# Reordering the passage into the first seven-product group of a two-layer encoder kernel

## The chip, the cores and the metric

The kernel runs on one core of one Trainium2 chip. The metric is the device time of one execution in microseconds, the median of several; smaller is better.

## The reference

Two layers, 256 tokens, model width 1024, float32 throughout. Each layer is a macaron: half a SwiGLU, a mixer of two attention groups, half a SwiGLU.

```python
for l in range(DEPTH):                      # DEPTH = 2, D_MODEL = 1024, D_FF = 2816
    x = x + 0.5 * swiglu(rms_norm(x, ffn1_norm[l]), w_gate1[l], w_up1[l], w_down1[l])
    h = rms_norm(x, mix_norm[l])
    qa, ka, va, qb, kb, vb = split(h @ w_in[l])
    x = x + concat(windowed_gqa_sink(...), differential_attention(...)) @ w_out[l]
    x = x + 0.5 * swiglu(rms_norm(x, ffn2_norm[l]), w_gate2[l], w_up2[l], w_down2[l])
return rms_norm(x, final_norm)
# swiglu(h) = (silu(h @ w_gate) * (h @ w_up)) @ w_down
```

So there are four SwiGLU blocks, called here F1 and F2 (layer 0) and F3 and F4 (layer 1), with a mixer between F1 and F2 and between F3 and F4. They hold nearly all of the arithmetic.

## The kernel before

**Matmuls in pieces.** Every float32 operand is cut into a high part, rounded to the matmul's format, and a low part, the rest; a product is three matmuls (high·high, low·high, high·low). A weight block of 4x128 rows by 512 columns is one *step*. It is loaded on SyncE's queue into one of six buffers (tag `raw`, `N_RAW = 6`) and then cut in two halves of 128x1024; each half, called a *split*, is one ScalarE cast (the high part) and one VectorE subtraction (the low part). Splits are numbered 2i and 2i+1 for step i. `emit_split` issues them; a raw buffer is given back when its second split has been done.

**Seven products for eight.** The hidden width is taken in groups of 512 columns, n = 0 to 4, and a rest of 256. A plain group multiplies two token halves by gate and up weights, each in two halves of the rows: eight products. For groups in `sevens`, `by_seven` uses a Strassen-like scheme with seven products. With a, d the two row halves of the gate block and b, c those of the up block, it needs the blocks a, d, c, b+c, a+b, a+b+c and a+b+c+d, and four sums of x (`make_sums`: s1, s2, b0_ and v, each with a high and a low part). F1 uses it for groups 2 to 4, the others for groups 1 to 4. Weight sums come about in two ways: `gather(k, to)` is a DMA on GpSimd's queue that reads block k from memory again and adds it into the buffer of block `to`; `plus(x, to)` is two VectorE additions of 128x1024 (tile `raw<-raw,raw`).

**Order.** Outside the attention part everything is kept in program order on each engine. The order is written by hand, by a planner: `weights()` hands out the next step and first calls `ahead(n)`, which issues all splits up to number n, the additions that lie between them, and the loads that now find a free buffer. n is `2 * i + look[0] - less`; `look[0]` is 8 or 7 in group 1. The columns of a step are handed out in two inner halves (`Split.part`); when a product reaches the second, `ahead` is called for one more split, unless the step was asked for with `held=True`. So the order of ScalarE and VectorE work is that of the calls of `weights()` in the source.

**Group 1 in F2, F3 and F4** (steps counted from the start of the SwiGLU block; group 0 uses steps 0 to 3): step 4 is a, 5 is d, 6 is the first half of the down projection of group 0, 7 is c, 8 is b+c, 9 is a+b, 10 is a+b+c, 11 is a+b+c+d, 12 is the other down half. Group 2 follows with step 13 (its a), 14 (its b+c) and so on. `by_seven` on the branch for g = 1 makes p1 (step 4), transposes the first half of the hidden tile `h` into `hT` (`turn`, tile `s`: TensorE transposes, a ScalarE cast, a VectorE subtraction), runs one part of `make_sums`, makes p2 (step 5), transposes the second half of `h`, runs the next part of `make_sums`, forms g0 = p1 + p2 and its silu, and goes on to the down projection (step 6), p3 (step 7), m7 (step 8), p5, p6 and p4 (steps 9 to 11) and step 12. Two VectorE instructions at the end of the group turn its products into the next `h`; the next group transposes it after its own first two products.

**Group 1 in F1** is the plain branch of the loop in `ffn`. There `make_sums` runs in five parts, one at each `next(sums)`: s1 and s2; their high parts; the low parts, b0_ and v; the high parts of b0_ and v; the low parts of these. v (tile `v`) is needed by the second product of group 2.

**Holding additions.** `issue(add)` keeps a gather back in `pending` while `hold[0]` is true, and `flush()` releases all. hold is set near the end of a SwiGLU block (`ffn_end`) and of the mixer, and flush comes after the statistics of the next norm have been issued (`norm.late(2)`, `take_x(2)`), so that GpSimd computes the norm's factor `r` before it takes up additions.

Of the kernel before, what the change touches and what calls it, by code (L numbers as in the profile page):

```python
# [12 lines left out]
ALU = mybir.AluOpType  # L13
# [21 lines left out]
def trunk(ctx: ExitStack, tc: tile.TileContext, x, n1, g1, u1, d1, nm, w_in, sink,  # L35
# [79 lines left out]
    def seven(wg, wu, c0, downs, first):  # L115

        a, b, c, d = [object() for _ in range(4)]  # L120
        w = {a: rows(wg, c0, 512, 0, 4), b: rows(wu, c0, 512, 0, 4), c: rows(wu, c0, 512, 4, 4), d: rows(wg, c0, 512, 4, 4)}

        def load(k):
            return lambda t: [(t, w[k])]

        def gather(k, to):
            def add():
                pool.dma_start(raws[to], w[k], accum_op=ALU.add)
            return add

        def plus(x, to):
            def prep():
                for h in (0, 2):
                    x_, t_ = [raws[i][:, h:h + 2] for i in (x, to)]
                    dve.tensor_tensor(t_, t_, x_, op=ALU.add)
            return prep

        bc = Step(4, 512, load(b), key=b, behind=gather(c, b))
        rest = [Step(4, 512, load(d), key=d, free=[]), Step(4, 512, load(c), key=c, free=[]), downs[0]]
        steps = [rest[0], rest[2], rest[1], bc] if first else [bc] + rest  # L140
        steps[0].prep = lambda: issue(gather(b, a))
        return [Step(4, 512, load(a), key=a, free=[])] + steps + [
                Step(4, 512, None, src=a, free=[]),
                Step(4, 512, None, prep=plus(c, a), src=a, free=[c]),
                Step(4, 512, None, prep=plus(d, a), src=a, free=[a, d]),
                downs[1]]

    def emit_dma(i):
        s = specs[i]
        raws[s.key] = raw = wp.tile([P, s.kn, s.n], F32, tag="raw", bufs=N_RAW, name=nm_("raw"))  # L150
        for dst, src in s.moves(raw):
            if i > 1:
                sp.dma_start(dst, src)  # L153
            else:
                for k in range(s.kn):
                    sp.dma_start(dst[:, k:k + 1], src[:, k:k + 1])
                    yield
        if s.behind is not None:
            issue(s.behind)


    pending, hold = [], [True]

    def issue(add):
        pending.append(add)
        if not hold[0]:
            flush()

    def flush():
        hold[0] = False  # L170
        while pending:
            pending.pop(0)()

# [73 lines left out]
    def weights(less=0, held=False):  # L247

        i = at["use"]
        at["use"] += 1  # L250
        if i > 1:
            ahead(2 * i + look[0] - less)
        w = loaded[i]
        w.held = held
        return w
# [179 lines left out]
    norm = Norm(0)  # L435
# [137 lines left out]
    class Residual:  # L573
# [5 lines left out]
        def add(self, h, t, c=None):  # L579
            a, b = (0, 512) if c is None else (c * 256, c * 256 + 256)  # L580
            xv = xk[:, t, h * 512 + a:h * 512 + b]
            dve.tensor_tensor(xv, xv, self.accs[h][t][:, a:b], op=ALU.add)
# [15 lines left out]
    def ffn(norm, aside=None, before=None, final=False, sevens=SEVEN[1]):  # L598
# [21 lines left out]
        def prod(xo, w):  # L620
            acc = bank()
            for k in range(4):
                hi, lo = w.part(k)
                xh, xl = xo(k)
                pe.matmul(acc, lhsT=xh, rhs=hi, start=k == 0, stop=False)
                pe.matmul(acc, lhsT=xl, rhs=hi, start=False, stop=False)
                pe.matmul(acc, lhsT=xh, rhs=lo, start=False, stop=k == 3)
            return acc

        def by_seven(h, g, sums):  # L630


            flat = lambda: tmp().rearrange("p a n -> p (a n)")

            def put(o, x, y, op):
                dve.tensor_tensor(o, x, y, op=op)
                return o

            m1, m7 = flat(), flat()
            if g > 1:  # L640
                act.copy(m1, prod(norm.quarter(0, 0), weights()))
                act.copy(m7, prod(norm.summed(3), weights(held=True)))
                hT = turn(h, 2)
                p2 = prod(norm.quarter(0, 1), weights())
                g0 = put(flat(), p2, m1, ALU.add)
                p3 = prod(norm.summed(2), weights())
                silu(g0, g0, 0)
                down(hT, g - 1, 0, weights())
            else:
                p1 = prod(norm.quarter(0, 0), weights())  # L650
                hT = turn(h, (0,))
                next(sums, None)
                w = weights()
                act.copy(m1, p1)
                p2 = prod(norm.quarter(0, 1), w)
                hT += turn(h, (1,))
                next(sums, None)
                w = weights()
                g0 = put(flat(), p2, m1, ALU.add)
                silu(g0, g0, 0)  # L660
                down(hT, 0, 0, w)
                p3 = prod(norm.summed(2), weights())
                act.copy(m7, prod(norm.summed(3), weights()))
            h = blk(F32)
            p5 = prod(norm.summed(0), weights())
            late = g == max(sevens)
            p6 = prod(norm.summed(1), weights(look[0] - 5 if late else 0, late))
            u2 = put(flat(), p6, m1, ALU.subtract)
            u3 = put(m7, m7, u2, ALU.add)
            p4 = prod(norm.quarter(1, 1), weights(look[0] - 4 if late else 0, late))  # L670
            g1 = put(m1, p4, u3, ALU.subtract)
            w = weights(look[0] - 3 if late else 0)
            silu(g1, g1, 1)
            put(u3, u3, p5, ALU.subtract)
            put(u2, u2, p5, ALU.subtract)
            put(u2, u2, p3, ALU.add)
            up(h, u2, g0, 0)
            up(h, u3, g1, 1)
            down(hT, g - 1, 1, w)
            return h  # L680

        def turn(hs, n):
            out_ = []
            for i in (range(n) if isinstance(n, int) else n):
                sl = halves(bank())
                for c in range(2):
                    for t in range(2):
                        pe.transpose(sl[:, c, t * P:(t + 1) * P], hs[:, t, (2 * i + c) * P:(2 * i + c + 1) * P], ident)
                hb = blk()
                split(hb, sl)  # L690
                out_.append(hb)
            return out_
# [3 lines left out]
        def down(hT, g, h, w):  # L696
            tokens(accs[h], [None] * (2 * g) + hT, w, 4 * g, last=(FC - 1, G4 - 1) if final and h else FC - 1)
# [14 lines left out]
        w = weights()  # L712
# [16 lines left out]
        for n in range(1, NGRP):  # L729
            if n in sevens:  # L730
                look[0] = IN_FFN + min(sevens) - n if before is not take_x else IN_MIX - (n == NGRP - 1)
                h = by_seven(h, n, sums)
                continue
            sums = norm.make_sums()
            gs = [bank(), bank()]
            tokens(gs, norm.xs, weights(), 0)
            hT = turn(h, 2)
            norm.copies()
            tokens(gs, norm.xs, weights(), 4)
            g = gate(gs)  # L740
            next(sums, None)
            us = [bank(), bank()]
            for k0 in (0, 4):
                tokens(us, norm.xs, weights(), k0)
                next(sums, None)
            h = hidden(g, us)
            for hh in range(2):
                down(hT, n - 1, hh, weights())
                next(sums, None)

        gu = [bank(), bank()]
        tokens(gu, norm.xs, weights(), 0)
# [14 lines left out]
    def ffn_end(parts, last):  # L767

        accs, hT, rest = parts
        hT = [None] * (2 * (NGRP - 1)) + hT  # L770
        hE = []
        look[0] = IN_MIX
        hold[0] = True
        w = {0: weights()}

        def group(h, order, a=None, c=slice(None), first=0):
            tokens(a or accs[h], hT, w[h], G4, first=first, last=last[h], order=order, cols=c)

        def tail(h, order=BY_TOKENS, a=None, c=slice(None)):
            tokens(a or accs[h], [None] * (2 * NGRP) + hE, w["rest"], 4 * NGRP, last=last[h], order=order, cols=c, h=h)  # L780

        group(0, [(k, t) for k in range(3) for t in range(2)])
        hE.extend(rest())
        group(0, [(3, t) for t in range(2)])
        w["rest"] = weights()
        w[1] = weights(2)
        return group, tail
# [20 lines left out]
    def mix(l, norm, nxt_norm):  # L808
# [215 lines left out]
        def out_part(w, k0, h, order=None):  # L1024
            tokens(accs[h], oT, w, k0, range(2), order=order, h=h)

        hold[0] = True
        for k0 in (0, 2, 4):
            w = weights()
            for h in range(2):  # L1030
# [112 lines left out]
```

## Time and profile before

| | |
|---|---|
| time, median of 3 runs | 942.56 us (942.45 to 946.13) |
| the profiled execution's own time | 946.32 us |
| its span, first to last instruction | 944.5 us |
| mean granted TensorE clock | 0.987 |
| TensorE busy | 916.6 us, 4696 matmuls |
| VectorE busy | 807.4 us, 1125 instructions |
| ScalarE busy | 590.6 us, 917 instructions |
| GpSimd busy | 65.3 us, 83 instructions |
| moved by DMA | 200.87 MB, mean 213 GB/s |

The profile is of one execution, in microseconds from its first instruction. Rows of a timeline give start, duration, engine, line, operation, output and input tiles (without buffer numbers), shapes, count and, in brackets, the idle time of the engine before it and what ended it. Nearly all instructions are issued through one helper at line 50, so tiles tell them apart: `w<-raw` is a split's cast (ACT) or subtraction (DVE), `s<-ps,s` the low part of `hT`, `q` and `v` are sums of x, `ps` is a PSUM bank. PE is TensorE, DVE VectorE, ACT ScalarE, POOL GpSimd, SPq SyncE's queue. The table of waits gives the time in total, the count and the longest. The table of stretches gives length, busy time of each engine with its count, granted TensorE clock, DMA share and rate. A row of DMA issues ends with the time from issue to landing. F1 lies at about 6 to 190 us of the span, F2 at 291 to 480, F3 at 481 to 662 and F4 at 763 to the end.

### The profile page before, as it was taken

The page shows a single profiled execution, that of the slowest core. Times are in us where ns is not written, and L with a number is a line of the kernel's source. Part 1 is how long each engine was busy: PE and PEld are TensorE (multiplying, and loading weights), DVE is VectorE, ACT ScalarE, POOL GpSimd, SP SyncE. Part 2 cuts the span into 40 slices and gives each one's busy share as a digit, 9 for nine tenths or more (in the row PEclk, how much of TensorE's full clock was granted, in tenths as well). Part 3 has the DMA queues.
Part 4 walks back from the last instruction along what each step waited for, and adds up shares of the span by engine and source line. Part 5 has one row for each costly group of instructions (what it writes and reads, how often), then busy time and mean ns, then how long its engine had stood idle before and what let it go on. Part 6 is the DMA issues. An engine that isn't in the chain of part 4 may idle for free.

```text
span 944.5 us, 12605 instructions
## 1 busy us (share of the span) xinstructions
PE 916.6 (97%) x4696; PEld 770.1 (82%) x4696; DVE 807.4 (85%) x1125; ACT 590.6 (63%) x917; POOL 65.3 (7%) x83
## 2 busy tenths in 40 slices
PE   8989999999999899999998999999999998999997
PEld 6778887899888688888886888888998886888886
DVE  6757999969885899999878999997788669999995
ACT  7835575647765765675484666665577485666661
POOL 0400010000000100100010010000001010010011
PEclk9998999999999999999998999999999999999999
DMA  9985897927434796897759897978472358898831
GB/s 341 353 209 135 266 279 252 271 90 223 135 110 158 179 283 192 255 294 247 262 145 220 242 275 206 275 256 235 119 237 91 133 137 221 254 262 227 247 146 45
DMA packets 114061, 200.87 MB, mean 213 GB/s; under 512 B 3662, under 2 KB 31376, under 8 KB 114000
## 3 DMA queue, kind: packets, MB, share of 16 engines
q1 hardware_dynamic: 96528, 166.74, 52.4%
q0 software_dynamic: 16096, 31.75, 18.7%
q10 hardware_dynamic: 1376, 1.57, 0.5%
q8 instruction: 37, 0.61, 0.3%
q14 instruction: 24, 0.20, 0.1%
HBM read 199.00 MB, written 1.05 MB: 212 GB/s over the span
## 4 chain that ended last, share of the span: by engine, by line
PE 71%; DMA 12%; DVE 7%; issue 6%; ACT 2%; POOL 0%; SPq 0%; ACTq 0%; POOLq 0%; DVEq 0%
PE ps L50 71%; DMA raw<-in_ffn_w_up_dram 10%; DVE w L50 4%; ACT w L50 1%; DMA raw<-in_ffn_w_gate_dram 1%; DVE raw L50 1%; DVE tmp L50 1%; DVE s L50 1%; DMA xk<-in_x_dram 1%; ACT s L50 0%; ACT junk L50 0%; ACT tmp L50 0%; DVE q L50 0%; POOL rb L50 0%; SPq L153 0%
## 5 line engine op out<-in xcount | busy, mean ns | idle before, releaser
L50 PE MATMUL ps<-w,s 128*128 128x512 f32 (+1 forms) x2574 | 608.0, 393 | 13.9 <-DVE s L50 12.7
L50 PEld LDWEIGHTS ps<-w,s 128*128 128x128 f32 x2574 | 480.8, 190 | 116.2 <-DVE s L50 15.0
L50 DVE TENSOR_TENSOR w<-raw,w 128x1024 fp32r<-128x1024 f32 (+1 forms) x458 | 483.4, 1099 | 48.4 <-ACT w L50 47.4
L50 ACT CAST w<-raw 128x1024 fp32r<-128x1024 f32 (+1 forms) x458 | 409.7, 952 | 124.2 <-DVE raw L50 85.1
L50 PE MATMUL ps<-w,q 128*128 128x512 f32 x540 | 127.6, 390 | 0.0
L50 PEld LDWEIGHTS ps<-w,q 128*128 128x128 f32 x540 | 101.7, 188 | 21.3
L50 PE MATMUL ps<-s,w 128*128 128x256 f32 x672 | 84.0, 285 | 0.0
L50 PEld LDWEIGHTS ps<-s,w 128*128 128x128 f32 x672 | 81.7, 191 | 1.1
L50 DVE TENSOR_TENSOR raw<-raw,raw 128x1024 f32<-128x1024 f32 x60 | 70.5, 1216 | 0.0
L50 POOL DMA_DIRECT2D raw<-in_ffn_w_up_dram x30 | 38.9, 1350 | 368.3 <-DVE w L50 127.5
L50 ACT ACTIVATE s<-ps,gcol 128x256 fp32r<-128x256 f32 (+1 forms) x80 | 31.3, 479 | 46.6 <-PE ps L50 45.0
L50 ACT ACTIVATE tmp<-tmp,r 128x512 f32<-128x512 f32 x30 | 21.7, 722 | 50.1 <-DVE tmp L50 50.1
L50 PE MATMUL ps<-w,v 128*128 128x512 f32 x180 | 45.9, 405 | 3.2 <-DVE v L50 3.2
L50 PEld LDWEIGHTS ps<-w,v 128*128 128x128 f32 x180 | 35.2, 196 | 11.1 <-DVE v L50 3.6
L50 PE MATMUL ps<-ident,s 128*128 128x128 f32 x304 | 41.3, 276 | 0.3 <-DVE s L50 0.3
L50 PEld LDWEIGHTS ps<-ident,s 128*128 128x128 f32 x304 | 35.9, 142 | 6.8 <-issue 1.0
L50 DVE TENSOR_TENSOR s<-ps,s 128x512 fp32r<-128x512 f32 x44 | 28.6, 682 | 10.5 <-ACT s L50 10.5
L50 ACT COPY tmp<-ps 128x512 f32<-128x512 f32 x34 | 19.9, 584 | 27.2 <-PE ps L50 25.6
L50 ACT CAST s<-ps 128x512 fp32r<-128x512 f32 x44 | 24.3, 591 | 20.2 <-PE ps L50 20.2
L50 ACT ACTIVATE s<-s,negm 128x256 f32<-128x256 f32 x64 | 31.9, 500 | 6.6 <-DVE negm L50 6.4
L50 DVE TENSOR_TENSOR tmp<-ps,tmp 128x512 f32<-128x512 f32 x49 | 33.4, 682 | 1.6 <-PE ps L50 1.6
L50 DVE SCALAR_TENSOR_TENSOR s<-ps,gcol,s 128x256 fp32r<-128x256 f32 x48 | 20.3, 478 | 14.8 <-ACT s L50 14.7
(106 smaller groups left out, 405.6 us busy)
## 6 DMA issues: line engine op xcount, KB each, us to landing
raw<-in_ffn_w_down_dram SPq DMA_DIRECT2D x44, 1024.0 KB, 6.5
raw<-in_ffn_w_gate_dram SPq DMA_DIRECT2D x39, 1024.0 KB, 6.5
raw<-in_ffn_w_up_dram SPq DMA_DIRECT2D x39, 1024.0 KB, 5.1
raw<-in_ffn_w_up_dram POOLq DMA_DIRECT2D x30, 1024.0 KB, 11.8
raw<-in_w_in_dram SPq DMA_DIRECT2D x14, 1024.0 KB, 5.4
raw<-in_ffn_w_gate_dram SPq DMA_DIRECT2D x8, 512.0 KB, 6.6
raw<-in_ffn_w_up_dram SPq DMA_DIRECT2D x8, 512.0 KB, 7.6
raw<-in_w_in_dram SPq DMA_DIRECT2D x8, 512.0 KB, 5.6
```

The source lines that it names most:

```text
L50: ins = issue(*a, **k)
```

## The change

Four edits, in four places.

1. In `by_seven` for g = 1, p1 and p2 ask for their steps with `weights(3, True)`: three splits fewer are issued before each product and none in its middle. The call of `weights()` for step 6 moves behind g0 and its silu, and g0 moves ahead of the last part of `make_sums`. Splits 15 to 20 and the additions for step 10 (with the one for split 17, the load of group 2's b) thus stand later in program order: split 15 after the first half of `hT`, the others behind the second half of `hT`, g0 and silu.
2. `hold` gets levels. The gather of c into b ("behind" a load) is kind 2 and is held only at the start of the kernel; the gather of b into a is kind 1 and is held as before.
3. In the plain group (F1, group 1), `next(sums)` is called once more, right after `norm.copies()`, so each part of `make_sums` runs one call earlier.
4. There, the call after the second down half is left out, since nothing remains to be done.

```diff
-        steps[0].prep = lambda: issue(gather(b, a))
+        steps[0].prep = lambda: issue(gather(b, a), 1)
...
         if s.behind is not None:
-            issue(s.behind)
-    pending, hold = [], [True]
-    def issue(add):
-        pending.append(add)
-        if not hold[0]:
-            flush()
+            issue(s.behind, 2)
+    pending, hold = [], [2]
+    def issue(add, kind):
+        if kind <= hold[0]:
+            pending.append(add)
+        else:
+            add()
     def flush():
-        hold[0] = False
+        hold[0] = 0
...
             else:
-                p1 = prod(norm.quarter(0, 0), weights())
+                p1 = prod(norm.quarter(0, 0), weights(3, True))
                 hT = turn(h, (0,))
                 next(sums, None)
-                w = weights()
+                w = weights(3, True)
                 act.copy(m1, p1)
                 p2 = prod(norm.quarter(0, 1), w)
                 hT += turn(h, (1,))
+                g0 = put(flat(), p2, m1, ALU.add)
                 next(sums, None)
-                w = weights()
-                g0 = put(flat(), p2, m1, ALU.add)
                 silu(g0, g0, 0)
-                down(hT, 0, 0, w)
+                down(hT, 0, 0, weights())
...
             norm.copies()
+            next(sums, None)
             tokens(gs, norm.xs, weights(), 4)
...
                 down(hT, n - 1, hh, weights())
-                next(sums, None)
+                if hh == 0:
+                    next(sums, None)
...
         look[0] = IN_MIX
-        hold[0] = True
+        hold[0] = 1
```

More of the change, by code (lines that the diff above doesn't have):

```diff
@@ L1025, in out_part @@
             tokens(accs[h], oT, w, k0, range(2), order=order, h=h)
-        hold[0] = True
+        hold[0] = 1
         for k0 in (0, 2, 4):
```

## The prediction

> **What bounds the kernel now.** I read the page's first part, then what TensorE waited for, then its timeline, and last the timelines of the engine that it waited for. On the page, TensorE is nearly always busy:
>
> ```profile
> PE 916.6 (97%) x4696; PEld 770.1 (82%) x4696; DVE 807.4 (85%) x1125; ACT 590.6 (63%) x917; POOL 65.3 (7%) x83
> ```
>
> The longest entry of its waits is for VectorE, tile `s`, the low parts of hT:
>
> ```profile
> PE ps L50 <- DVE s L50: 13.0, 7, 3.1
> ```
>
> Its timeline shows where. In F1, group 2's second product (right operand `v`) starts and stops:
>
> ```profile
> 67.37 0.39 PE L50 MATMUL ps<-w,v 128*128 128x512 f32 x1
> 70.96 5.06 PE L50 MATMUL ps<-w,v 128*128 128x512 f32 x11 [3.20 <-DVE v L50]
> 77.17 2.99 PE L50 MATMUL ps<-w,s 128*128 128x512 f32 x12
> ```
>
> In F2, group 1's down projection stops twice, and F3 and F4 repeat it. The two last rows are transposes of a hidden tile: group 2's and, two groups on, group 4's.
>
> ```profile
> 322.18 0.48 PE L50 MATMUL ps<-w,s 128*128 128x512 f32 x1
> 324.45 3.06 PE L50 MATMUL ps<-w,s 128*128 128x512 f32 x12 [1.79 <-DVE s L50]
> 330.07 4.13 PE L50 MATMUL ps<-w,s 128*128 128x512 f32 x11 [2.56 <-DVE s L50]
> 334.03 2.88 PE L50 MATMUL ps<-w,q 128*128 128x512 f32 x12
> 358.51 1.03 PE L50 MATMUL ps<-ident,s 128*128 128x128 f32 x8
> 420.17 1.04 PE L50 MATMUL ps<-ident,s 128*128 128x128 f32 x8
> ```
>
> A wait costs more than itself. The stretches show the granted clock (the first figure behind the five engines) at half after each:
>
> ```profile
> 71.00:72.00 1.00, 1.00 (x3) 0.81 (x4) 1.00 (x1) 0.00 (x0) 0.00 (x0) 0.50 0.00 0
> 330.00:332.00 2.00, 1.93 (x5) 1.55 (x6) 2.00 (x4) 0.00 (x0) 0.69 (x1) 0.50 0.74 129
> ```
>
> So F1 lost between 67.37 and 77.17: 9.80 us for twelve matmuls (2.99 by the row at 77.17) and eight transposes (1.03 by the row at 358.51), that is 5.8 too many, of which 3.2 were the wait and 2.6 the slow clock. F2 lost 334.03 - 322.18 = 11.85 us for 24 matmuls, worth 2 x 2.99: 5.9 too many.
>
> Whether that can be had depends on VectorE, which TensorE waits for. Its timeline in F2, from split 15 on:
>
> ```profile
> 320.31 3.49 DVE L50 TENSOR_TENSOR w<-raw,w 128x1024 fp32r<-128x1024 f32 x3
> 323.71 0.68 DVE L50 TENSOR_TENSOR s<-ps,s 128x512 fp32r<-128x512 f32 x1
> 325.92 1.23 DVE L50 TENSOR_TENSOR w<-raw,w 128x1024 fp32r<-128x1024 f32 x1 [0.21 <-ACT w L50]
> 334.74 1.23 DVE L50 TENSOR_TENSOR w<-raw,w 128x1024 fp32r<-128x1024 f32 x1 [1.79 <-ACT w L50]
> 338.22 9.23 DVE L50 TENSOR_TENSOR w<-raw,w 128x1024 fp32r<-128x1024 f32 x8
> 354.73 1.42 DVE L50 SCALAR_TENSOR_TENSOR s<-tmp,hr,tmp 128x512 f32<-128x512 f32 x2
> 359.82 1.29 DVE L50 TENSOR_TENSOR s<-ps,s 128x512 fp32r<-128x512 f32 x2 [0.27 <-ACT s L50]
> 418.09 1.42 DVE L50 SCALAR_TENSOR_TENSOR s<-tmp,hr,tmp 128x512 f32<-128x512 f32 x2
> ```
>
> The row at 354.73 finishes group 1's hidden tile at 356.15, 2.36 before TensorE transposes it at 358.51. The row at 418.09 finishes group 3's at 419.51, only 0.66 before 420.17. From 320.31 to 419.51 VectorE stood idle for hardly more than the brackets 0.21, 1.79 and 0.27. In these groups VectorE is the engine that is full; TensorE's waits at 322 to 330 are mostly matters of order, and what it gains there it can lose again at the next hidden tile.
>
> **Part by part: F1** (one part of the sums earlier, four small steps of ScalarE and VectorE moved, none added). VectorE there:
>
> ```profile
> 59.07 2.36 DVE L50 TENSOR_TENSOR w<-raw,w 128x1024 fp32r<-128x1024 f32 x2 [10.97 <-ACT w L50]
> 65.08 4.62 DVE L50 TENSOR_TENSOR w<-raw,w 128x1024 fp32r<-128x1024 f32 x4
> 70.22 0.68 DVE L50 TENSOR_TENSOR v<-tmp,v 128x512 fp32r<-128x512 f32 x1
> 77.53 1.29 DVE L50 TENSOR_TENSOR s<-ps,s 128x512 fp32r<-128x512 f32 x2 [5.49 <-ACT s L50]
> ```
>
> The low part of v stands behind four splits and ends at 70.90. One call earlier, the four sum instructions that followed 59.07 fall into the 10.97 of idle time ahead of it, and v's low part stands behind only two of the four splits: 59.07 + 2.36 + 1.42 (hidden tile) + 2.31 (half of 4.62) + 2 x 0.68 = 66.5, against 67.37 when the product starts. The wait goes, with a margin of 0.9. VectorE had itself waited 5.49 for the next hT, so it has room to follow, and the loads behind follow it. Term: **-5.8**, between -3.2 (only the wait) and -6.3 (rows overlap by some tenths).
>
> Here one rule bears. The Trainium skill, "TensorE: Matmul & The Clock Gate", section "What's actually happening", says that the clock halves after an idle window of about 3.4 us. By that rule a wait of 3.20 us would cost no clock, and this term would be -3.2, the whole change 940.0 us. The trace disagrees: after 3.20 and even after 2.56 us of idle time the granted clock was 0.50.
>
> **F2, the order in group 1.** After the change hT's first low part comes before splits 15 to 17 (at about 320.3 instead of 323.71) and its second before splits 16 to 19 and the two additions for step 10. Both are then ready when the down projection wants them; both waits go. But VectorE does the same work by the time of its hidden tile. It loses the idle 0.21 and 1.79, and gets new gaps: split 15 must wait for its cast, which now starts after hT's, and split 16 for a cast behind the silu of g0. I put these at 1.1 and 0.6 from the casts' 0.96 (6.75 / 7, next fence) and the 0.68 of the sums; bounds 0 and 1.8 each. So VectorE comes out 0.3 earlier, no more.
>
> Then there is the queue behind split 17. The planner loads group 2's b into the buffer that split 17 gives back, and the gather of c follows the load:
>
> ```profile
> 323.82 0.37 SPq L153 DMA_DIRECT2D raw<-in_ffn_w_up_dram  x1
> 329.40 1.28 POOL L50 DMA_DIRECT2D raw<-in_ffn_w_up_dram  x1 [18.92 <-DVE raw L50]
> raw<-in_ffn_w_up_dram SPq DMA_DIRECT2D x1, 1024.0 KB, 5.0
> raw<-in_ffn_w_up_dram POOLq DMA_DIRECT2D x1, 1024.0 KB, 10.8
> raw<-in_ffn_w_up_dram POOLq DMA_DIRECT2D x1, 1024.0 KB, 12.2
> 341.66 6.75 ACT L50 CAST w<-raw 128x1024 fp32r<-128x1024 f32 x7
> ```
>
> The load is issued at 323.82, as split 17 ends (320.31 + 3.49). The gather goes out 5.6 later and lands 10.8 after that, at 340.2. Split 28, the third of the seven casts from 341.66, needs it at 343.6: 3.4 in hand. After the change split 17 ends at about 328.6 (320.31, then hT 0.64, gap 1.1, split 1.16, hT, g0 and two sums 2.5, gap 0.6, two splits 2.3). Load and gather start 4.8 later: the gather goes out at 334.2. It now runs beside the loads of d, c and a down block, as does the gather that took 12.2 in the next group; I take 11.5, the middle of 10.8 and 12.2. It lands at 345.7, the cast ends at 346.75, and VectorE wanted it at 338.22 - 0.3 + 6 x 1.15 = 344.8. VectorE then waits 2.0 (1.25 to 2.65 by the two rows), and group 1's hidden tile comes at 356.15 - 0.3 + 2.0 = 357.85. TensorE, at hand some 6 us earlier, waits for it, partly already for PSUM banks that VectorE frees late. From there VectorE does not have to wait the 0.27 again, and group 3's tile comes at 419.51 + 1.7 - 0.27 = 420.9 against the 420.17 of before: **+0.8**.
>
> The new stall may again halve the clock: 0 to 2.6. From 357.85, two groups (420.17 - 358.51 = 61.66) would bring TensorE to 419.5, 1.4 ahead of VectorE, so only what exceeds 1.4 counts: 0 to 1.2. I take 0.
>
> **F3 and F4** have the same stalls, and more room:
>
> ```profile
> 540.53 1.23 DVE L50 TENSOR_TENSOR w<-raw,w 128x1024 fp32r<-128x1024 f32 x1 [0.36 <-ACT w L50]
> 542.80 1.29 DVE L50 TENSOR_TENSOR s<-ps,s 128x512 fp32r<-128x512 f32 x2 [1.04 <-ACT s L50]
> 600.90 1.42 DVE L50 SCALAR_TENSOR_TENSOR s<-tmp,hr,tmp 128x512 f32<-128x512 f32 x2
> 603.15 1.03 PE L50 MATMUL ps<-ident,s 128*128 128x128 f32 x8
> 823.46 1.29 DVE L50 TENSOR_TENSOR s<-ps,s 128x512 fp32r<-128x512 f32 x2 [0.58 <-ACT s L50]
> 881.54 1.41 DVE L50 SCALAR_TENSOR_TENSOR s<-tmp,hr,tmp 128x512 f32<-128x512 f32 x2
> 883.81 1.04 PE L50 MATMUL ps<-ident,s 128*128 128x128 f32 x8
> ```
>
> F3: 1.7 less the idle 1.40 and the margin 603.15 - 602.32 = 0.83: **-0.5**. F4: 1.7 - 0.58 - (883.81 - 882.95): **+0.3**.
>
> **Gathers not held.** The load of b is issued well ahead of the flush:
>
> ```profile
> 292.04 0.37 SPq L153 DMA_DIRECT2D raw<-in_ffn_w_up_dram  x1
> 307.83 2.65 POOL L50 DMA_DIRECT2D raw<-in_ffn_w_up_dram  x2
> ```
>
> With 5.0 for the load, c is added from about 297 instead of 307.83, so GpSimd is free again when it must compute `r`, and the flush finds one gather instead of two. It would shorten the wait for splits 16 and 18, but edit 1 has moved these to 325 and later: worth nothing beside it, 0. If the load landed after 307, `r` would wait behind it on GpSimd; 10 us of room speak against it.
>
> **Sum.** -5.8 + 0.8 - 0.5 + 0.3 = -5.2 on a span of 944.5, whose execution took 946.32. The median, 942.56, lies 3.8 below that execution, and nothing shows where; I take the difference over unchanged: 942.56 - 5.2 = 937.4.
>
> **The rivals.**
>
> *All waits become time* (0.05): 5.8 + 3 x 5.9 = 23.5, 919 us. For it: the waits are named and the edit removes them. Against: VectorE's margin of 0.66 at group 3's tile.
>
> *The gather is in time* (0.20): it lands in 10.8 and the gaps are small, so each passage is better by 0.75 and part of the 1.7 of gaps; some 1.8 each, -10.6, 932 us. For it: the row of this very place took 10.8. Against: the loads that now fall beside it.
>
> *Given back* (0.25): the gather takes 12.2 and the cold clock counts 0.6 in each passage, 3 x (0.65 + 0.6) = 3.8, 941 us (0.20); or the slow clock in F1 comes back at another place, so that only its wait is gained, 940 us (0.05). The skill's rule above would give this last time too. For it: TensorE must wait somewhere, if VectorE is full. Against: 1.4 of room for a slow clock.
>
> *Slower* (0.08): one mechanism, the delayed gather at split 28. Every us that it lands later is a us of VectorE in each of three passages. At 15.5 us instead of 11.5 it costs 12, and 942.56 - 5.2 + 12 = 949 us; from 13.2 on the gain is gone. Of the rows above none is over 12.2.
>
> That an edit does nothing is so for the gathers above; if the sums in F1 still came too late (by more than the margin 0.9), that term would shrink to the lower bound, which is in the third rival.
>
> **How the numbers follow.** The forecast, 934.9 to 939.9, has 0.42, of which 0.33 below 937.8. A measurement here can tell about 0.5%, 4.7 us. Faster by more: 0.33 + 0.20 + 0.05 = 0.58. Within: 0.09 + 0.25 = 0.34. Slower: 0.08. The range runs from the second rival, 931, to the worst of the third with both ends of gather and clock, 942.5; it leaves out the first and the last rival and small tails.
>
> **What would show it.** In the changed profile TensorE should no longer wait for `v` in F1, nor for `s` in the down projection at 322 to 330. It should wait instead at the transposes of group 2, for the hidden tile, by several us. ScalarE should wait for a DMA in front of split 28, with VectorE behind it. TensorE's total wait would fall by less than the 16 us it had. I am wrong if the transposes of group 2 come 5 us earlier than now without a wait (VectorE had slack that I missed), or if group 2's first gather lands before ScalarE asks.

## The result, and the profile after

The changed kernel takes 940.24 us (median of 6 runs, 938.79 to 940.8), the kernel before 944.72 beside it (6 runs, 942.45 to 946.13). The ratio is 0.9955 (95% interval 0.994 to 0.9971), that is 0.45% or 4.3 us less, where 5.2 less was forecast. The profiled execution took 939.61, its span is 937.8 against 944.5, and the mean granted clock is 0.997 against 0.987.

The page's first line after the change. TensorE is busy 3.5 less, with most of the slow clock gone; the other engines' times are within 1.6 of what they were:

```profile
PE 913.1 (97%) x4696; PEld 764.6 (82%) x4696; DVE 807.4 (86%) x1125; ACT 590.4 (63%) x917; POOL 66.9 (7%) x83
```

What TensorE waits for now. The entry for `v` is gone, that for `s` has fallen from 13.0 to 4.1 in more and shorter pieces, and a new one has come: `tmp`, PSUM banks that VectorE reads late.

```profile
PE ps L50 <- DVE tmp L50: 6.8, 5, 2.6
PE ps L50 <- DVE s L50: 4.1, 11, 0.8
PE ps L50 <- DVE w L50: 1.9, 4, 0.5
```

TensorE's timeline in F1 after. The product with `v` runs its twelve matmuls without a stop, and the matmuls that began at 77.17 begin at 71.40, 5.77 earlier:

```profile
67.88 2.89 PE L50 MATMUL ps<-w,v 128*128 128x512 f32 x12
71.40 3.01 PE L50 MATMUL ps<-w,s 128*128 128x512 f32 x12
```

TensorE's timeline in F2 after. The down projection of group 1 runs through (24 matmuls in one row at 316.08). The waits now stand in front of group 2's hidden tile. The last three rows are group 4's transposes, the end of group 4, where TensorE waits 0.46 for a split, and the transposes of the rest:

```profile
316.08 5.74 PE L50 MATMUL ps<-w,s 128*128 128x512 f32 x24
...
342.22 2.97 PE L50 MATMUL ps<-w,s 128*128 128x512 f32 x12 [1.27 <-DVE tmp L50]
345.82 2.97 PE L50 MATMUL ps<-w,v 128*128 128x512 f32 x12 [0.63 <-DVE tmp L50]
349.56 0.33 PE L50 MATMUL ps<-ident,s 128*128 128x128 f32 x1 [0.77 <-DVE s L50]
350.22 0.98 PE L50 MATMUL ps<-ident,s 128*128 128x128 f32 x7 [0.33 <-DVE s L50]
...
412.75 1.30 PE L50 MATMUL ps<-ident,s 128*128 128x128 f32 x8
...
431.33 13.45 PE L50 MATMUL ps<-w,s 128*128 128x512 f32 x58 [0.46 <-DVE w L50]
444.62 1.03 PE L50 MATMUL ps<-ident,s 128*128 128x128 f32 x8
```

VectorE's timeline in F2 after. The brackets are the new gaps: 1.03 before split 15, 0.59 before split 16, 0.49 before split 28. The fourth row finishes group 1's hidden tile, the last one cuts four splits of group 4:

```profile
315.93 1.23 DVE L50 TENSOR_TENSOR w<-raw,w 128x1024 fp32r<-128x1024 f32 x1 [1.03 <-ACT w L50]
320.15 4.63 DVE L50 TENSOR_TENSOR w<-raw,w 128x1024 fp32r<-128x1024 f32 x4 [0.59 <-ACT w L50]
339.11 2.36 DVE L50 TENSOR_TENSOR w<-raw,w 128x1024 fp32r<-128x1024 f32 x2 [0.49 <-ACT w L50]
348.75 1.42 DVE L50 SCALAR_TENSOR_TENSOR s<-tmp,hr,tmp 128x512 f32<-128x512 f32 x2
430.05 4.70 DVE L50 TENSOR_TENSOR w<-raw,w 128x1024 fp32r<-128x1024 f32 x4
```

Behind the 0.49 stands the gather, issued at 328.12 on GpSimd's queue and landing 9.8 later, with ScalarE's cast waiting for it:

```profile
328.12 1.28 POOL L50 DMA_DIRECT2D raw<-in_ffn_w_up_dram  x1 [25.11 <-DMA raw<-in_ffn_w_up_dram]
raw<-in_ffn_w_up_dram POOLq DMA_DIRECT2D x1, 1024.0 KB, 9.8
338.03 4.84 ACT L50 CAST w<-raw 128x1024 fp32r<-128x1024 f32 x5 [0.93 <-DMA raw<-in_ffn_w_up_dram]
```

In F3 the same gather took 11.2: VectorE loses 1.81 there, and TensorE waits 2.56 in one piece, after which twelve matmuls take 4.58.

```profile
521.87 2.36 DVE L50 TENSOR_TENSOR w<-raw,w 128x1024 fp32r<-128x1024 f32 x2 [1.81 <-ACT w L50]
524.98 4.58 PE L50 MATMUL ps<-w,s 128*128 128x512 f32 x12 [2.56 <-DVE tmp L50]
```

**Where the time went.** As a mark in each block I take the start of the transposes in front of the rest of 256 columns. It moves from 170.37 to 164.28 in F1, from 451.09 to 444.62 in F2, from 633.99 to 627.47 in F3, and from 914.66 to 907.92 in F4. So F1 gives 6.09, and the three passages together 0.65 (0.38, 0.05 and 0.22). In this pair of executions the change is F1 and little else.

### The profile page after: what moved, and what is told of

It is laid out like the page before. It is cut to its first block, busy times and chain, and to the rows that moved or that the text cites. A ratio compares the mean times of both kernels' runs of the same rounds, so it can differ in the third digit from the quotient of the medians.

```text
span 937.8 us, 12599 instructions
## 1 busy us (share of the span) xinstructions
PE 913.1 (97%) x4696; PEld 764.6 (82%) x4696; DVE 807.4 (86%) x1125; ACT 590.4 (63%) x917; POOL 66.9 (7%) x83
## 4 chain that ended last, share of the span: by engine, by line
PE 56%; DVE 20%; DMA 12%; ACT 6%; issue 4%; POOLq 0%; ACTq 0%; POOL 0%; DVEq 0%
PE ps L50 56%; DVE w L50 12%; DMA raw<-in_ffn_w_up_dram 12%; ACT w L50 4%; DVE tmp L50 4%; DVE raw L50 2%; DVE s L50 2%; ACT s L50 1%; ACT tmp L50 1%; DMA xk<-in_x_dram 1%; ACT junk L50 0%; ACT q L50 0%; ACT L50 0%; DVE q L50 0%; ACT v L50 0%
## 5 line engine op out<-in xcount | busy, mean ns | idle before, releaser
L50 PEld LDWEIGHTS ps<-ident,s 128*128 128x128 f32 x304 | 34.8, 140 | 14.2 <-DVE s L50 9.4
L50 PE MATMUL ps<-w,v 128*128 128x512 f32 x180 | 43.5, 391 | 1.2 <-DVE tmp L50 1.2
L50 DVE TENSOR_TENSOR tmp<-tmp,ps 128x512 f32<-128x512 f32 x45 | 29.5, 683 | 0.5
## 6 DMA issues: line engine op xcount, KB each, us to landing
raw<-in_ffn_w_up_dram POOLq DMA_DIRECT2D x30, 1024.0 KB, 11.8
```

Of the source, the lines that this page charges most:

```text
L50: ins = issue(*a, **k)
```

## The experiments

Theory A is that of the prediction: in the passages VectorE is full, so that a wait of TensorE that goes comes back at the next hidden tile, and only VectorE's own idle time can be won. Its rival D: TensorE, or the transfers, bound the passages, and VectorE has room. What else was held against A is spelled out in the expectations.

**The parts alone and in pairs.** The first has edits 3 and 4 of the change:

```diff
             norm.copies()
+            next(sums, None)
...
-                next(sums, None)
+                if hh == 0:
+                    next(sums, None)
```

> Only the two edits in F1 (sums one call earlier), the rest as before. Theory A (VectorE is full in F2 to F4, so the reordering there nets little, and F1 carries the change): 5.5 to 6.3 us faster than before, hardly less than the whole change, and the passages of F2 to F4 with their old waits. Rival B (the waits removed in group 1 of F2 to F4 are time, F1's is made up for later): under 3 us faster.

939.76 against 946.20: 0.9937 (0.9914 to 0.9961). The wait for `v` is gone, and the waits for `s` are there as before (12.5 us). F1 alone gives as much as the whole change.

The second has edits 1 and 2, F1 as before (`weights(3, True)`, step 6 asked for behind silu, and the levels of `hold`; two lines of it):

```diff
-                p1 = prod(norm.quarter(0, 0), weights())
+                p1 = prod(norm.quarter(0, 0), weights(3, True))
...
-            issue(s.behind)
+            issue(s.behind, 2)
...
```

> Only the edits in group 1 of F2 to F4 (later splits and the gather not held), F1 as before. Theory A: 0 to 1.5 us faster; TensorE's waits move from the down projection of group 0 to the products and transposes at the start of group 2. Rival B: 4 us faster or more.

944.72: 0.9989 (0.9976 to 1.0002), which can't be told from no change. TensorE's waits in F2 to F4 moved as they did in the whole change; F1's stayed:

```profile
PE ps L50 <- DVE tmp L50: 6.3, 5, 2.2
PE ps L50 <- DVE s L50: 3.5, 8, 0.8
PE ps L50 <- DVE v L50: 3.2, 1, 3.2
```

The third is the change without edit 2, the fourth is the kernel before with edit 2 alone (one line of the edit stands for all of it):

```diff
-            issue(s.behind, 2)
+            issue(s.behind)
...
```

> The whole change without the gather's release: both gathers are held until the flush, as before. Theory A: as the whole change within 0.5 us, since split 16 is now asked for after both have landed. Rival C (the release is what keeps the reordering from waiting for the gathers): 1 to 4 us slower than the whole change, with a wait of ScalarE for a DMA in front of split 16 or 18.

```diff
-            issue(s.behind)
+            issue(s.behind, 2)
...
```

> Only the gather's release, all else as before. Theory A: the gather into a lands some 5 us earlier, so split 18 does not hold ScalarE up any more; that takes 0.2 us of idle time from VectorE in F2 and F4 and 1.3 in F3, so 0 to 1.7 us faster than before. Rival C (an addition that runs beside the loads near the end of the block delays these): slower by 1 us or more.

Without edit 2: 939.56, 0.9935 (0.9912 to 0.9958), no worse than the change. Edit 2 alone: 941.86, 0.9954 (0.9941 to 0.9968), 4.3 us less, which I had not expected. In F2 its gather goes out at 296.13, before `r` is computed at 305.80, split 18's cast finds its data, and VectorE's gaps of 0.2 to 1.1 in front of splits 18 and 19 in F2 to F4 are gone. In the profiled executions 3.1 of the gain lies between F1's mark and F4's. The prediction saw that this wait goes and gave it nothing beside edit 1; what it didn't ask is whether edit 1 is worth having.

That was tried later, with the kernel before plus edits 2, 3 and 4 (the order of group 1 as before), and the change itself again beside it:

```diff
-                p1 = prod(norm.quarter(0, 0), weights(3, True))
+                p1 = prod(norm.quarter(0, 0), weights())
...
-                w = weights(3, True)
+                w = weights()
...
-                g0 = put(flat(), p2, m1, ALU.add)
                 next(sums, None)
+                w = weights()
+                g0 = put(flat(), p2, m1, ALU.add)
                 silu(g0, g0, 0)
-                down(hT, 0, 0, weights())
+                down(hT, 0, 0, w)
```

> The two edits in F1 and the gather's release, with the old order in group 1 of F2 to F4. Theory A (VectorE's idle time between the first sums and group 2 is what counts, not TensorE's waits): F1's 5.9 us and the 3 us or so that the release alone gave in F2 to F4 add up, 8 to 10 us faster than before and 3 to 5 faster than the whole change, although TensorE's long waits in the down projection are all still there. Rival B (the waits count): slower than the whole change.

```diff
 (the changed kernel as it is)
```

> The whole change once more, on the chip of the three others and beside the same runs of before: 4 to 6 us faster than before.

935.60 against 946.77: 0.988 (0.986 to 0.9899); the change 940.91: 0.9932 (0.9915 to 0.9949). The intervals do not meet: edit 1 costs about 5 us where it stands beside edit 2 (3.1 and 4.9 by the marks, in the table below). It costs nothing measurable without it (the first run against the third).

**Is VectorE the bound?** The next two leave out VectorE's additions for the weight sums in F2 to F4, but for those for step 10 in group 1, first in the changed kernel, then in the one before:

```diff
...
-                Step(4, 512, None, prep=plus(c, a), src=a, free=[c]),
-                Step(4, 512, None, prep=plus(d, a), src=a, free=[a, d]),
+                Step(4, 512, None, prep=plus(c, a) if first or f1 else None, src=a, free=[c]),
+                Step(4, 512, None, prep=plus(d, a) if f1 else None, src=a, free=[a, d]),
```

> The whole change with less VectorE work in F2 to F4: of the additions of 128x1024 between buffers, those of group 1's step 10 stay (they belong to the reordered part), all the others there are left out, so the sums a+b+c+d and, in groups 2 to 4, a+b+c are not formed. That is 2.35 us less in each group 1 and 4.7 less in each group 2 to 4. Theory A (VectorE bounds groups 1 to 4): the waits at the start of group 2 shrink from some 4 us to under 1 in each of F2 to F4, TensorE keeps the lead, and the kernel is 20 us or more faster than before (5.9 of F1 and about 5 in each passage). Rival D (TensorE's new waits come from the late gather or the PSUM banks, not from VectorE's work): the waits stay, 7 to 9 us faster than before.

> The kernel before with the same additions left out. Theory A: TensorE was bound by the waits in group 1 and not by VectorE afterwards, so little comes of it: 0 to 3 us faster than before (the small waits at group 4 go), and the distance to the changed kernel with the same omission is 17 us or more. Rival D: the same 0 to 3 us, but a distance of 7 us or less.

The changed kernel: 922.91 against 945.03, 0.977 (0.9745 to 0.9795), with TensorE's work unchanged; its wait at group 2's transposes in F2 is 0.26 and 0.34, and there is none for `tmp`. The same bytes were moved in less time, so neither TensorE nor the rate of the transfers bound the passages, and rival D falls. The run isn't free of other effects: with the additions gone buffers come free earlier, and the stalls for the gather in front of split 28 went as well. But VectorE's gaps shrank by only 3.2 us (9.0 to 5.8), while the marks of F1 and F4 moved 16.7 closer to each other (743.6 to 726.9).

The kernel before got slower: 957.39, 1.0134 (1.0109 to 1.0158). With the additions gone, buffers come free earlier, two loads are issued beside the two held gathers, and these take 14.2. In the old order split 18's cast stands in front of that of hT's second half on ScalarE, and hT waits with it:

```profile
raw<-in_ffn_w_up_dram POOLq DMA_DIRECT2D x2, 1024.0 KB, 14.2
326.52 1.05 ACT L50 CAST w<-raw 128x1024 fp32r<-128x1024 f32 x1 [4.54 <-DMA raw<-in_ffn_w_up_dram]
328.90 0.59 ACT L50 CAST s<-ps 128x512 fp32r<-128x512 f32 x1
...
333.18 4.69 PE L50 MATMUL ps<-w,s 128*128 128x512 f32 x11 [3.15 <-DVE s L50]
```

So the control isn't clean: it took work away and moved the transfers. It shows what a late gather costs in these passages, a mechanism like that of the prediction's fourth rival, but at split 18 and in the old order.

**VectorE's work given to GpSimd**, in the changed kernel: one addition of 128x512 per group, or the low part of one split per group, 15 instructions each.

```diff
-            u3 = put(m7, m7, u2, ALU.add)
+            u3 = m7
+            pool.tensor_tensor(m7, m7, u2, op=ALU.add)
```

> The whole change with one sum of each seven-product group, u3 = m7 + u2 (128x512), on GpSimd instead of VectorE. Theory A: VectorE is relieved of 0.6 us a group; by group 4 of F2 to F4 that adds up to 2.4 us each and to 1.8 in F1 if TensorE can use it, so 3 to 8 us faster than the whole change. Against it: GpSimd's addition takes about 1.3 us where VectorE takes 0.69, and g1 waits for it; if that wait stands in VectorE's queue, nothing is gained or up to 1 us a group is lost. Rival D: no gain.

```diff
...
-            dve.tensor_tensor(l_, r_, f(h_), op=ALU.subtract)
+            (pool if (i, j) in aside_ else dve).tensor_tensor(l_, r_, f(h_), op=ALU.subtract)
```

> The whole change with the low part of one split of each seven-product group (the first half of its second down block, wanted late) on GpSimd instead of VectorE. Theory A: VectorE is relieved of 1.15 us a group, and nothing waits for GpSimd's 2.6 us or so; by group 4 that is up to 4.6 us in each of F2 to F4, of which TensorE can use what it now waits, so 5 to 12 us faster than the whole change. Rival D: no gain. If GpSimd and VectorE hinder each other, VectorE's splits beside it take longer than 1.15 us each.

945.67, 1.0007 (0.9993 to 1.0022), and 950.89, 1.0063 (1.0042 to 1.0085): some 5 and 10 us more than the change takes by its first ratio. Two rows of the first one's timelines, VectorE's and GpSimd's, and the two groups of GpSimd's additions in it:

```profile
342.50 3.44 DVE L50 TENSOR_TENSOR w<-raw,w 128x1024 fp32r<-128x1024 f32 x2
342.67 2.18 POOL L50 TENSOR_TENSOR tmp<-tmp,tmp 128x512 f32<-128x512 f32 x1 [2.57 <-DVE tmp L50]
L50 POOL TENSOR_TENSOR tmp<-tmp,tmp 128x512 f32<-128x512 f32 x15 | 30.9, 2062 | 127.2 <-DVE tmp L50 127.2
L50 POOL TENSOR_TENSOR xk<-xk,s 128x512 f32<-128x512 f32 x2 | 2.6, 1293 | 12.6 <-DVE tot L50 12.6
```

The two splits took 3.44 beside the addition, where two take 2.36 (the row at 339.11). VectorE's busy time rose from 807.4 to 809.8 with 15 instructions fewer. Both engines are held up, so this is no test of theory A: VectorE was not relieved.

**A half order, and silu later.** Under theory A the best order is the one that leaves VectorE no gap, whatever TensorE waits for. In the changed kernel, p1 asks for its step as in the kernel before, only one split is held back at p2, and silu follows the down projection, so that split 16's cast isn't behind it; then silu's place alone:

```diff
-                p1 = prod(norm.quarter(0, 0), weights(3, True))
+                p1 = prod(norm.quarter(0, 0), weights())
...
-                w = weights(3, True)
+                w = weights(1, True)
...
-                silu(g0, g0, 0)
                 down(hT, 0, 0, weights())
+                silu(g0, g0, 0)
```

> A version of the change: in group 1 of F2 to F4 only splits 18 and later move behind the second half of hT, splits 15 to 17 stay ahead of the first, and the silu of g0 moves behind the down projection. Theory A: VectorE then has none of the gaps (1.0 and 0.6 in front of splits 15 and 16, 1.8 in front of split 21), so it is 2 us ahead in each passage, split 17 gives its buffer back as early as before, TensorE keeps its first wait of 1.8 and loses the second: 11 to 13 us faster than before, 6 to 8 faster than the whole change. Rival B: no better than the whole change, for one of the two waits is back.

```diff
-                silu(g0, g0, 0)
                 down(hT, 0, 0, weights())
+                silu(g0, g0, 0)
```

> The whole change with only the silu of g0 moved behind the down projection. Theory A: the gap of VectorE in front of split 16 (0.6) goes, since its cast need not wait for g0; 0 to 2 us faster than the whole change over three passages. Rival B: no difference.

The half order: 929.04, 0.9809 (0.9793 to 0.9826), 17.7 us less than before and more than I had expected; it beats both kernels. The order was not run with silu in its old place. Silu alone: 938.07, 0.9911 (0.9893 to 0.9928), an interval that meets that of the change; in F2 VectorE's gap in front of split 16 went, but the one in front of split 28 was 1.78. The half order's timeline in F2, TensorE's and VectorE's. TensorE still waits 1.80 at the old place, VectorE has no bracket from group 0's hidden tile (309.76) to group 1's (345.63), and group 2's transposes come without a wait:

```profile
317.63 5.51 PE L50 MATMUL ps<-w,s 128*128 128x512 f32 x23 [1.80 <-DVE s L50]
347.47 1.03 PE L50 MATMUL ps<-ident,s 128*128 128x128 f32 x8
309.76 1.41 DVE L50 SCALAR_TENSOR_TENSOR s<-ps,hr,tmp 128x512 f32<-128x512 f32 x2
...
329.12 9.23 DVE L50 TENSOR_TENSOR w<-raw,w 128x1024 fp32r<-128x1024 f32 x8
...
345.63 1.42 DVE L50 SCALAR_TENSOR_TENSOR s<-tmp,hr,tmp 128x512 f32<-128x512 f32 x2
```

**Ten profiles in one table.** All ten have the same work on every engine. The first figure is VectorE's idle time in the passages: the brackets of its timeline in F2, F3 and F4, each from group 0's hidden tile to the low parts of group 2's hT, added up (in F2 of the kernel before: 0.21, 1.79 and 0.27). The second is the time from the mark of F1 to that of F4, which leaves F1 out.

| kernel | VectorE's gaps, us | F1's mark to F4's, us |
|---|---|---|
| half order | 0 | 733.7 |
| before + edits 2, 3, 4 | 6.4 | 740.6 |
| before + edit 2 | 7.0 | 741.2 |
| before + edits 1, 2 | 8.5 | 742.6 |
| the change | 9.0 | 743.6 |
| the change without edit 2 | 9.1 | 744.0 |
| before | 9.6 | 744.3 |
| the change, silu later | 10.0 | 743.9 |
| the change again | 10.6 | 745.5 |
| before + edits 3, 4 | 11.8 | 747.0 |

A us of gap is about a us of time: the second figure less the first lies between 733.7 and 735.2 in all ten. One kernel's order can differ by some 2 us of gap between executions (the change and the change again; before, with and without edits 3 and 4, which touch F1 alone), so only the larger steps tell kernels apart. TensorE's own waits, added up over the same stretch, follow the time less closely: they are 5.8 in the half order and 9.5 to 12.9 in the others, and the time less these waits lies between 727.9 and 734.1. The change again waits 12.0, less than the 12.3 of the change, and takes 1.8 longer. A single wait tells nothing: in the half order TensorE waits 1.80 at one place of F2, in the change never so long there, and the half order is the faster by 10 us.

## Why the prediction was right or wrong

**F1, -5.8: right.** The mark moved by 6.09, the matmuls behind the stall by 5.77. v was ready at 66.2 (65.48 + 0.68, the row below), where 66.5 was forecast.

```profile
65.48 0.68 DVE L50 TENSOR_TENSOR v<-tmp,v 128x512 fp32r<-128x512 f32 x1
```

By the rule of the Trainium skill's page "TensorE: Matmul & The Clock Gate", section "What's actually happening", only 3.2 of this could have been won. The trace disagrees: more than the wait was won, since the slow clock behind it went too.

**That TensorE's waits are mostly order: right.** They moved to where they were forecast, the hidden tile of group 2, in F2 with 1.90 of 3.00 us as waits for PSUM banks. The two new gaps before splits 15 and 16 measured 1.03 and 0.59 in F2, against 1.1 and 0.6.

**The gather: too dear in F2, right in F3.** Forecast was 11.5 from issue to landing and a stall of 2.0 in every passage; it was 9.8 and 0.49 in F2, 11.2 and 1.81 in F3, 10.3 and 0.93 in F4. The gather went out when forecast: 328.12 is 1.28 before the 329.40 of the kernel before, and with F1's 6.09 taken off 4.8 later. With the hidden tile 1.5 earlier than in the sum, F2's +0.8 becomes -0.7.

**The step that failed: where the sum ended.** The prediction stopped at group 4's transposes and credited TensorE with its margin there. They did come 7.42 earlier (420.17 to 412.75), 1.3 more than F1 gives, better even than -0.7. One group on, at the mark, 0.4 was left. VectorE's splits in group 4 show why. Before, the row stood at 436.54, and TensorE ran through the end of the group without a wait:

```profile
436.54 4.71 DVE L50 TENSOR_TENSOR w<-raw,w 128x1024 fp32r<-128x1024 f32 x4
437.41 13.84 PE L50 MATMUL ps<-w,s 128*128 128x512 f32 x60
```

After, VectorE's row stands at 430.05, earlier by 6.49, which is F1 and 0.4, and TensorE, which was further ahead, waits 0.46 for a split (the row at 431.33). The splits of group 4 leave no more room than the 0.4, so what the passages win is VectorE's gaps before less its gaps after, 9.6 - 9.0 = 0.6 (0.65 by the marks), and not what TensorE finds at an early transpose. By that rule the forecast's own gaps, 3 x (1.1 + 0.6 + 2.0) = 11.1, would have cost 1.5 where it put +0.6. The sum of -5.2 came near by luck: gaps of the new order taken too large, idle time of the old order taken too small (F2's 2.0 and 1.40 in F3, where the rows of its timeline add up to 4.5) and margins wrongly credited went opposite ways. The measured 0.45% falls in the prediction's class "within", to which it gave 0.34, and not in "faster by more", to which it gave 0.58.

**Gathers not held, 0: right for the sum, wrong for the kernel.** Edit 2 is worth 4.3 us alone by the medians and nothing beside edit 1. The table fits a reason: edit 2 takes gaps of VectorE away, edit 1 puts others in their place.

**The rivals.** "All waits become time" fell with the result. "The gather is in time" held in part in F2, where the gather took 9.8, but the passage gave 0.38 and not 1.8. The change's median of 940.24 is near the time of "given back", but not by its mechanism: the gathers took 9.8 to 11.2 and not 12.2, F1 kept its gain, and in F2 the slow clock was not there after the short waits (granted clock 1.00 from 342 to 351). In F3 it was: the twelve matmuls that took 4.58.

**What stays open.** The change won 6.7 us between the two profiled executions, 4.5 between the first medians, and 5.9 between the last. Executions of the kernel before spread from 942.1 to 949.3. Between the two profiled executions of the change the stall in front of split 28 in F4 alone differs by 1.5 (0.93 and 2.41); why a gather lands later in one execution than in another was not looked into. The slow clock behind F1's stall differs between executions (eleven matmuls took 5.06 in one, 3.88 in another), and that may be another part; it was not tried by itself.

## What to carry to other kernels

Before reordering to remove the waits of the busiest engine, look at who finishes last at the next point where the two engines meet; if that is the other engine, first add up the gaps of that one before and after; its work must be the same in both. A cast or a transfer that is ready late should stand behind, not ahead of, the small steps that others wait for, and the queue needs something ready to fill the gap: holding one split back, with silu behind the products, did that here; holding three back made new gaps. And try an edit's parts singly: here, by the medians, one part was worth 6 us, one 4, and the third took the second away.

## What the runs showed of the hardware that was not expected

**A wait's length alone does not decide whether the clock falls.** At the same place of F2, after the same wait of 1.80, the granted clock from 319 to 321 was 0.50 in one kernel (before with edits 2, 3 and 4) and 1.00 in the other (the half order):

```profile
319.00:321.00 2.00, 2.00 (x6) 1.59 (x5) 2.00 (x3) 0.01 (x1) 0.00 (x0) 0.50 1.02 393
319.00:321.00 2.00, 2.00 (x11) 1.64 (x10) 2.00 (x3) 0.00 (x0) 0.00 (x0) 1.00 1.02 392
```

**VectorE and GpSimd hold each other up** on float32 additions and subtractions: GpSimd's addition took 2.06 us beside splits, 1.29 beside none, and the two splits 1.09 more. The Trainium skill's page "SBUF — State Buffer", section "Who interferes with whom", says that a VectorE instruction with two inputs in SBUF and a GpSimd instruction that reads SBUF block each other whole, the later one waiting. The rows fit it: if GpSimd, issued at 342.67, waits for the first split to end at about 343.66 (342.50 + 1.16) and then takes 1.29, it ends at 344.95, against 344.85 measured, and the second split would end at about 346.1, against 345.94. Where GpSimd came first, in the run that gave it low parts, the rows fit too:

```profile
438.52 2.47 POOL L50 TENSOR_TENSOR w<-raw,w 128x1024 fp32r<-128x1024 f32 x1 [26.36 <-ACT w L50]
439.41 2.67 DVE L50 TENSOR_TENSOR w<-raw,w 128x1024 fp32r<-128x1024 f32 x1 [0.68 <-ACT w L50]
```

VectorE's subtraction, worth about 1.16, ends at 442.08, 1.09 after GpSimd's end at 440.99, as if it had begun only then. No run shows that it is this lock and nothing else.
